# A decoder trunk on one core: the forget gate's columns in V's tiles, recurrent gates in plain float32, and another list for attention's entry

## The chip, the cores and the metric

The kernel runs on one core of one Trainium2 chip. A core has TensorE (in the views PE for its matmuls, PEld for its weight loads), VectorE (DVE), ScalarE (ACT), GpSimd (POOL) and SyncE (SP), which issues most DMAs. The metric is the time of one execution in device microseconds. The time of before is the median of three runs.

## The reference

Two layers over 256 positions of 1024 features. Each layer is a half-step SwiGLU FFN (1024 to 2816 and back), a token mixer and a second FFN, each with an RMS norm before and after it. The mixer of layer 0 is recurrent, that of layer 1 is attention with a forget gate, whose K, V and gate sum come from the stream between the layers.

```python
# layer 0's mixer; 1344 channels, 16 blocks of 84
gate, rec = split(hn @ w_in)
rec = causal_depthwise_conv(rec, conv_w, conv_b)           # 4 taps
r = sigmoid(blockwise(rec, w_a) + b_a);  i = sigmoid(blockwise(rec, w_x) + b_x)
log_a = -8 * r * softplus(-lam);  a = exp(log_a)
u = sqrt(-expm1(2 * log_a)) * (i * rec)
h_t = a_t * h_(t-1) + u_t                                   # a scan over the positions
m = (gelu(gate) * h) @ w_out
# shared by layer 1, from z = rms_norm(h, kv_norm_g)
k, v = split(z @ w_kv);  c = cumsum(log_sigmoid(z @ w_f + b_f))    # w_f: 1024 x 16
# layer 1's mixer, causal, 16 heads of 64
logits = q k^T / 8 + c_q - c_k;  m = softmax(logits) v @ w_o
```

## The kernel before, in words

**Split matmuls.** A float32 weight tile `raw` (128 x up to 1024) is split by `split` (L169) into a high part `whi`, which ACT copies with rounding to float32r (L178), and a low part `wlo`, which DVE gets by subtraction (L179). Activations are split in the same way (`xhi`, `xlo`; `zhi`, `zlo`; `hhi`, `hlo`; `yh`, `yl`). `mm3` (L184 to L188) forms a product from three float32r matmuls with the activation stationary: hi by hi, hi by lo, lo by hi. `mm3w` (L190 to L195) does so with the weight stationary. Attention's logits (L970) and values (L997) are plain float32 matmuls.

**Items and slots.** The weights form a list of items; each has a `prep` (load and split) and a `work` for the token tiles t = 0 and t = 1 (128 positions each). `slot(t, i)` does one item's work and then a `tick`. `run` lets t = 0 go ahead of t = 1 by up to `LAG` = 7 items. There are 3 buffers for raw tiles and 10 for split ones (`RAW`, `WB`); `prepare_next` prepares an item when the one ten before it is done for both token tiles. A tick counts down what `defer(n, fn)` has postponed by n ticks, prepares an item and issues some of `queue`, in which each entry has a cost in us; up to `SHARE` = 0.8 us of cost is issued per tick, and `flush(key)` issues all up to the last entry of a key. The order of PE's instructions is that of the program; the order of the other engines is set by a scheduler when the kernel is built.

**Ends of sub-layers.** `row_items` (L395) runs the products that go back to 1024 columns, in two PSUM banks of 512 columns. For t = 1 its last `rows` items are done bank by bank. Then `enter` (L247) takes square sums of both banks (ACT, L208), rstd (POOL, L201 and L203), adds to the stream `h` (DVE, L260), and defers the transposes and splits that make the next inputs: `inputs` by 3 ticks (L217), or `norm`, by 1 tick, which normalises h first (`stat`, then `hn`, L277) and defers the transposes `go` (L284) by 2 more. `norm` is used at the end of the first FFN, ahead of the recurrent stage.

**The recurrent stage** follows a list written by hand, `RG_ORDER` (L818): `0g3` is gate unit 3 for t = 0 (columns of `gate`, in groups of 504, 504 and 336; 2 or 3 k-tiles per unit), `r2` makes two 126-channel tiles of `rec` for all 256 positions, `gw2` is the blockwise gates of that pair. `conv` (L631): ACT writes `xc` from PSUM, DVE adds three taps (L647), ACT makes `ch` (L649), DVE `cl` (L652). A gw unit loads eight small blocks, splits them as a weight tile, does 8 products of 256 columns with `mm3w` and takes tanh (L694). `after_gates` queues L711 (scale and shift, DVE), tanh (L714), exp (L715), L716 and a Newton step (L720 to L725) for expm1's accuracy. For every two pairs `batch` queues the square roots (L739), u (L744, L745), the scans (L749), the transposes of the gate columns (L757) and their gelu (L759), the product (L771), and its split (`yh` L773, `yl` L778). `w_out` follows as `row_items` whose row k needs batch k // 4.

**K, V and the forget gate.** `post_f` and `work_f` (L897, L933): V's first half as four items of 512 columns, the forget gate as one item with 16 columns and 8 k-tiles, V's second half, then K. Both read `zx`, which `enter` of the second FFN makes as the first of two destinations.

**Attention** follows `ATT_ORDER` (L1045): `0` and `1` are the next item of that token tile (8 of w_q, then 8 of w_o), `a0` and `a1` the next step of the attention of that tile. Step i issues logits i, values i - 3, transposes i - 2 and, at two places, an output. `heads_T` (L869) makes q's transposes by deferring two `turn`s by 2 and 3 ticks.

Of the kernel before, what the change touches and what calls it, by code (L numbers as in the profile page):

```python
# [44 lines left out]
def trunk_kernel(ctx: ExitStack, tc: tile.TileContext, A: dict, out: bass.AP):  # L45
# [201 lines left out]
    def enter(t, dests, pf, gb, half, last=False, normed=False):  # L247
# [24 lines left out]
        def norm():  # L272
            stat(t)
            hn = []
            for n in range(2):
                hn.append(hpool.tile([P, 512], F32, tag="t1", name=nm("hn"), bufs=2))
                nc.vector.tensor_scalar(hn[n], h[t][:, n * 512:(n + 1) * 512], rs[t][:, 0:1], None, ALU.mult)  # L277

            def go():
                tps = []  # L280
                for n in range(2):
                    tp = gtbank()
                    for j in range(4):
                        nc.tensor.transpose(tp[:, j * P:(j + 1) * P], hn[n][:, j * P:(j + 1) * P], ident)  # L284
# [110 lines left out]
    def row_items(w, widths, get_x, post, rows=1):  # L395


        acc = {}
        kept = []
        nk = len(widths)  # L400
        r0 = 0
        for k, kp in enumerate(widths):
            def prep(kp=kp, r0=r0):
                return split(load_raw(w[r0:r0 + kp, :], kp, D), kp, D)

            def work(t, u, k=k):
                if k == 0:
                    acc[t] = [mmbank(), mmbank()]
                if t == 1 and k >= nk - rows:
                    kept.append((k, u))  # L410
                    if k < nk - 1:
                        return
                    todo = [(kk, uu, n) for n in range(2) for (kk, uu) in kept]
# [19 lines left out]
    def ffn_items(pool_of, wg, wu, wd, post_g, next_dests, last=False, normed=False):  # L433
# [55 lines left out]
        row_items(wd, [P] * 22, lambda t, k: (hid[t][0][:, k, :], hid[t][1][:, k, :]), post_down, 4 if last else 1)  # L489
# [46 lines left out]
    sp2 = rw.tile([RT, NRT], F32, name="sp2")  # L536

# [7 lines left out]
    def rg_params():  # L545
# [8 lines left out]
        def rest():  # L554
# [3 lines left out]
            nc.vector.tensor_scalar(sp2, sp, 2.0, None, ALU.mult)  # L558
        defer(1, rest)

# [14 lines left out]
    xcs, chs, tt, th, yy = {}, {}, {}, {}, {}  # L575

    def add_gate_unit(g, k0, kn):
# [5 lines left out]
        def work(t, u):  # L583
# [6 lines left out]
            if k0 + kn == 8:  # L590
                tok = pools["r"].tile([P, 4 * RT], F32, tag="tok", name=nm("tok"), bufs=4)
                nc.scalar.activation(tok[:, :nn], ps, AF.Copy)
                toks[(g, t)] = tok
# [37 lines left out]
    def conv(p, ps):  # L631
        tl, w = tiles_of(p), pw(p)
        m = len(tl)
# [3 lines left out]
        ch = pools["r"].tile([RT, 2, S], F32R, tag="ch", name=nm("ch"), bufs=2)  # L637
        cl = pools["r"].tile([RT, 2, S], F32R, tag="cl", name=nm("cl"), bufs=2)
        xcs[p], chs[p] = xc, (ch, cl)
# [4 lines left out]
        def taps(j, i):  # L644
# [4 lines left out]
            nc.scalar.activation(ch[:w, j, :], xc[:w, j, :], AF.Copy)  # L649

        def low():
            nc.vector.tensor_tensor(cl[:w, :m, :], xc[:w, :m, :], ch[:w, :m, :].bitcast(F32), ALU.subtract)  # L652

        first = [(1.25, ("c", p), lambda j=j, i=i: taps(j, i)) for j, i in enumerate(tl)] + [(0.65, ("c", p), low)]
# [3 lines left out]
    def add_gw_unit(p):  # L658
        tl, w = tiles_of(p), pw(p)
        m = len(tl)  # L660
        n = m * RT if m == 2 else BLK

        def prep():
            raw = new_raw()
            v = raw[:w, :2 * m * n]
# [11 lines left out]
            return split(v, w, 2 * m * n)  # L677

        def work(t, u):
# [3 lines left out]
            ch, cl = chs[p]  # L683
# [16 lines left out]
        rg[f"gw{p}"] = len(items)  # L700
        items.append((prep, work))

    def after_gates(p):
# [3 lines left out]
        t_ = tt[p][:w, :m, :] if p in tt else None  # L707

        def zz():
            for j, i in enumerate(tl):  # L710
                nc.vector.tensor_scalar(th[p][0][:w, j, :], th[p][0][:w, j, :], sp2[:w, i:i + 1], sp2[:w, i:i + 1],  # L711
                                        ALU.mult, ALU.add)
            tt[p] = pools["r"].tile([RT, 2, S], F32, tag="tt", name=nm("tt"), bufs=6)
            nc.scalar.activation(tt[p][:w, :m, :], z, AF.Tanh)  # L714
            nc.scalar.activation(z, z, AF.Exp, scale=-2.0)  # L715
# [3 lines left out]
        def newton():  # L719
            nc.vector.tensor_scalar(z, z, 0.5, 0.5, ALU.mult, ALU.add)  # L720
            nc.vector.scalar_tensor_tensor(b, tt[p][:w, :m, :], 1.0, z, ALU.add, ALU.mult)
# [6 lines left out]
        queue.extend([(1.1 * s, ("n", p), zz), (1.0 * s, ("n", p), newton), (1.0 * s, ("n", p), newton2)])  # L728
# [3 lines left out]
    def batch(g):  # L732

        pairs = [p for p in (2 * g, 2 * g + 1)]

        def roots():
            for p in pairs:
                v = tt[p][:pw(p), :len(tiles_of(p)), :]
                nc.scalar.activation(v, v, AF.Sqrt)  # L739

        def u_of(p):
            w, m = pw(p), len(tiles_of(p))
            v = tt[p][:w, :m, :]
# [3 lines left out]
        def scan(p, j):  # L747
            w = pw(p)
            nc.vector.tensor_tensor_scan(tt[p][:w, j, :], th[p][0][:w, j, :], tt[p][:w, j, :], 0.0, ALU.mult, ALU.add)  # L749

        def gelu(t):
            tok = toks[(g, t)]
            tp = trbank()
            y = pools["r"].tile([RT, 4, P], F32, tag="y", name=nm("y"), bufs=2)
# [3 lines left out]
            for (a, b, w) in parts_of(g):  # L758
                nc.scalar.activation(y[:w, a:b, :], tp[:w, a * P:b * P].rearrange("p (a b) -> p a b", a=b - a),  # L759
                                     AF.Gelu_apprx_tanh)  # L760
            ys[(g, t)] = y

        def product(t):
            y = ys[(g, t)]
            if t not in yy:
                yy[t] = (pools["r"].tile([RT, NRT, P], F32R, name=f"yh{t}"), pools["r"].tile([RT, NRT, P], F32R, name=f"yl{t}"))
            yh, yl = yy[t]
            for jj, p in enumerate(pairs):
                w, m = pw(p), len(tiles_of(p))
                v = y[:w, 2 * jj:2 * jj + m, :]  # L770
                nc.vector.tensor_tensor(v, v, tt[p][:w, :m, t * P:(t + 1) * P], ALU.mult)  # L771
            for (a, b, w) in parts_of(g):
                nc.scalar.activation(yh[:w, 4 * g + a:4 * g + b, :], y[:w, a:b, :], AF.Copy)  # L773

        def low(t):
            y, (yh, yl) = ys[(g, t)], yy[t]
            for (a, b, w) in parts_of(g):
                nc.vector.tensor_tensor(yl[:w, 4 * g + a:4 * g + b, :], y[:w, a:b, :],  # L778
                                        yh[:w, 4 * g + a:4 * g + b, :].bitcast(F32), ALU.subtract)
# [7 lines left out]
        q.insert(2, (0.0, key, lambda: gelu(0)))  # L787
        q.insert(3, (0.0, key, lambda: gelu(1)))
# [5 lines left out]

    ys = {}
# [7 lines left out]
    add_rec_units(0)  # L803
    add_rec_units(1)
    add_gw_unit(0)
    add_rec_units(2)
    add_gw_unit(1)
    add_rec_units(3)
    add_gw_unit(2)
    for k0 in (0, 3, 6):  # L810
        add_gate_unit(2, k0, min(3, 8 - k0))
    add_rec_units(4)
    add_gw_unit(3)
    add_rec_units(5)
    add_gw_unit(4)
    add_gw_unit(5)
# [11 lines left out]
    def get_yy(t, k):  # L828
        flush(("y", k // 4))
        w = width(k)  # L830
        return yy[t][0][:w, k, :], yy[t][1][:w, k, :]
# [60 lines left out]
    def post_v(n):  # L892
        def f(t, ps):
            nc.scalar.activation(kv["v"][t][:, n * 512:(n + 1) * 512], ps, AF.Copy, scale=rs[t][:, 0:1])
        return f

    def post_f(t, ps):  # L897
# [8 lines left out]
        def rest():  # L906
# [5 lines left out]
            defer(9, lambda: running(t))  # L912
# [13 lines left out]
    proj_items(A["w_kv"], D, 512, z_x, post_v(0))  # L926

    def prep_f():
        raw = new_raw()
        nc.sync.dma_start(raw[:, :P].rearrange("p (k n) -> p k n", k=8), A["w_fgate"].rearrange("(k p) n -> p k n", p=P))  # L930
        return split(raw[:, :P], P, P)

    def work_f(t, u):  # L933
        ps = mmbank()[:, :NH]
        for k in range(8):
            mm3(ps, *z_x(t, k), u.hi[:, k * NH:(k + 1) * NH], u.lo[:, k * NH:(k + 1) * NH], k == 0, k == 7)
        post_f(t, ps)

    items.append((prep_f, work_f))
    proj_items(A["w_kv"], D + 512, 512, z_x, post_v(1))  # L940
# [92 lines left out]
    for n in range(2):  # L1033
# [11 lines left out]
    ATT_ORDER = ("0 0 0 0 0 0 0 0 a0 1 a0 1 1 a0 1 a0 1 a0 1 a0 1 a0 a1 1 a0 a1 "  # L1045
                 "0 a1 0 a1 0 a1 0 a1 0 a1 0 a1 0 a1 0 a1 1 a1 1 a1 1 1 1 1 1 1")
# [29 lines left out]
    run(n_ffn1, lag_in=3)  # L1076
# [3 lines left out]
    for name in RG_ORDER:  # L1080
# [8 lines left out]
        else:  # L1089
            slot(None, rg[name])  # L1090
    state["a"] = state["b"] = n_rg
    run(n_wout)
# [61 lines left out]
```

## Time and profile before

| | |
|---|---|
| median of 3 runs (lowest to highest) | 1058.16 us (1056.62 to 1058.39) |
| the profiled execution: time, span | 1056.71 us, 1055.0 us |
| mean granted TensorE clock | 0.982 |
| first FFN ends, t = 0 and t = 1 | about 199 and 211 us |
| recurrent stage with w_out | about 211 to 346 us |
| V, forget gate and K | about 534 to 597 us |
| attention with w_q and w_o | about 781 to 861 us |

The span is the time from the first instruction to the last; 1.7 us of the execution lie outside it. Busy shares say how long an engine had an instruction in it. Matmuls are pipelined: a record of 0.39 us can be followed by the next after 0.23 us, so the rate of PE is read from one start to the next. "A <- B: x, n, m" in a list of waits says that A's engine sat idle for x us in all, n times, at longest m, until B was done. A granted clock of 0.90 over a stretch says that the throttle let TensorE have nine tenths of its full clock there, as a mean.

### The profile page before, as it was taken

To read this page: it belongs to the slowest core of one execution; us is meant where nothing else is said; L and a number is where in the kernel's file an instruction comes from. 1 tells how busy PE (TensorE), PEld (TensorE's weight loads), DVE (VectorE), ACT (ScalarE), POOL (GpSimd) and SP (SyncE) were. 2 spreads that over 40 slices of the span, in tenths; PEclk is the share of its full clock that TensorE was granted. 3 is DMA by queue.
4 is the path that set the end of the run, shared out by engine and by line. 5 is a ranking of instruction groups with operands and counts; after the bars stand their busy time and mean duration, and the time that the engine had idled before them with its cause. 6 is when DMAs were issued, how large, how long until landed. Compare 5 with 4: busy or idle time off the path is not lost.

```text
span 1055.0 us, 13090 instructions
## 1 busy us (share of the span) xinstructions
PE 1019.9 (97%) x4870; PEld 843.2 (80%) x4870; DVE 624.0 (59%) x771; ACT 539.3 (51%) x739; POOL 48.7 (5%) x109
## 2 busy tenths in 40 slices
PE   7999999989978999999999999999999999999997
PEld 4778888779966888888878888888888888888885
DVE  4666554548997755554486455555476475555542
ACT  3555543538886644443355444444357574454431
POOL 4200000010001100000010000000010010000000
PEclk9999999989988999999999999999999999999999
DMA  5776655536245676655446666655563156766541
GB/s 185 236 221 196 182 188 189 160 88 161 70 158 161 203 213 192 183 181 195 142 160 181 178 180 180 195 182 184 190 203 113 49 161 178 200 180 189 190 140 40
DMA packets 90742, 178.86 MB, mean 170 GB/s; under 512 B 11694, under 2 KB 28150, under 8 KB 90678
## 3 DMA queue, kind: packets, MB, share of 16 engines
q1 hardware_dynamic: 90006, 177.94, 55.9%
q8 instruction: 38, 0.62, 0.2%
q14 instruction: 26, 0.21, 0.1%
q0 software_dynamic: 640, 0.07, 0.1%
q10 hardware_dynamic: 32, 0.01, 0.0%
HBM read 176.95 MB, written 1.05 MB: 169 GB/s over the span
## 4 chain that ended last, share of the span: by engine, by line
PE 83%; DVE 6%; ACT 4%; DMA 4%; issue 2%; POOL 1%; DVEq 0%; SPq 0%; POOLq 0%; ACTq 0%
PE mm L186 25%; PE mm L188 25%; PE mm L187 25%; DVE wlo L179 3%; PE tr L462 2%; DMA raw<-in_ffn_w_gate_dram 2%; ACT whi L178 1%; PE mm L997 1%; PE gt L970 1%; ACT junk L208 1%; DMA raw<-in_ffn_w_up_dram 1%; PE gt L217 1%; PE tr L883 1%; PE mm L195 1%; PE mm L193 1%
## 5 line engine op out<-in xcount | busy, mean ns | idle before, releaser
L179 DVE TENSOR_TENSOR wlo<-raw,whi 128x1024 fp32r<-128x1024 f32 (+3 forms) x338 | 408.0, 1210 | 312.8 <-ACT whi L178 307.6
L178 ACT ACTIVATE whi<-raw 128x1024 fp32r<-128x1024 f32 (+2 forms) x332 | 348.6, 1052 | 359.9 <-PE mm L188 290.9
L186 PE MATMUL mm<-whi,xhi 128*128 128x512 f32 (+2 forms) x784 | 312.3, 398 | 5.3 <-ACT xhi L229 3.3
L187 PE MATMUL mm<-wlo,xhi 128*128 128x512 f32 (+2 forms) x784 | 306.4, 391 | 1.5 <-DVE wlo L179 1.5
L188 PE MATMUL mm<-whi,xlo 128*128 128x512 f32 (+2 forms) x784 | 306.5, 391 | 0.0
L186 PEld LDWEIGHTS mm<-whi,xhi 128*128 128x128 f32 x784 | 148.6, 189 | 35.2 <-POOL whi L176 3.4
L188 PEld LDWEIGHTS mm<-whi,xlo 128*128 128x128 f32 x784 | 148.3, 189 | 31.7 <-DVE xlo L232 0.6
L187 PEld LDWEIGHTS mm<-wlo,xhi 128*128 128x128 f32 x784 | 148.7, 190 | 30.5 <-DVE wlo L179 2.1
L186 PE MATMUL mm<-whi,hhi 128*128 128x512 f32 x352 | 139.5, 396 | 0.0
L188 PE MATMUL mm<-whi,hlo 128*128 128x512 f32 x352 | 139.0, 395 | 0.0
L187 PE MATMUL mm<-wlo,hhi 128*128 128x512 f32 x352 | 138.7, 394 | 0.0
L188 PEld LDWEIGHTS mm<-whi,hlo 128*128 128x128 f32 x352 | 66.1, 188 | 15.4
L187 PEld LDWEIGHTS mm<-wlo,hhi 128*128 128x128 f32 x352 | 66.1, 188 | 15.3
L186 PEld LDWEIGHTS mm<-whi,hhi 128*128 128x128 f32 x352 | 66.1, 188 | 15.1
L456 DVE SCALAR_TENSOR_TENSOR prod<-mm,rstd,sil 128x512 f32<-128x512 f32 (+1 forms) x48 | 33.9, 705 | 37.8 <-PE mm L188 34.0
L447 ACT ACTIVATE sil<-mm,rstd 128x512 f32<-128x512 f32 (+1 forms) x48 | 31.3, 651 | 44.9 <-PE mm L188 44.9
L201 POOL TENSOR_SCALAR nv<-ss 128x1 f32<-128x1 f32 x24 | 9.4, 391 | 759.6 <-ACT junk L208 759.6
L256 DVE TENSOR_TENSOR t<-mm,gb 128x512 f32<-128x512 f32 x24 | 16.3, 688 | 31.1 <-ACT junk L208 30.8
L466 ACT ACTIVATE hhi<-tr 128x512 fp32r<-128x512 f32 (+1 forms) x48 | 26.6, 553 | 14.6 <-PE tr L462 14.5
L467 DVE TENSOR_TENSOR hlo<-tr,hhi 128x512 fp32r<-128x512 f32 (+1 forms) x48 | 30.5, 642 | 3.4 <-ACT hhi L466 1.5
L208 ACT ACTIVATE junk<-mm 128x512 bf16<-128x512 f32 x24 | 14.2, 592 | 33.2 <-PE mm L188 32.8
L186 PE MATMUL mm<-whi,zhi 128*128 128x512 f32 (+1 forms) x80 | 31.0, 387 | 0.0
(178 smaller groups left out, 950.7 us busy)
## 6 DMA issues: line engine op xcount, KB each, us to landing
raw<-in_ffn_w_down_dram SPq DMA_DIRECT2D x88, 512.0 KB
raw<-in_ffn_w_up_dram SPq DMA_DIRECT2D x80, 512.0 KB
raw<-in_ffn_w_gate_dram SPq DMA_DIRECT2D x78, 512.0 KB
raw<-in_rg_w_in_dram SPq DMA_DIRECT2D x20, 504.0 KB
raw<-in_w_kv_dram SPq DMA_DIRECT2D x16, 512.0 KB
raw<-in_ffn_w_gate_dram SPq DMA_DIRECT2D x20, 256.0 KB
raw<-in_rg_w_out_dram SPq DMA_DIRECT2D x10, 504.0 KB
raw<-in_ffn_w_up_dram SPq DMA_DIRECT2D x16, 256.0 KB
```

What stands on the lines that cost most here:

```text
L178: nc.scalar.activation(hi[:parts, c:c + m], rawv[:, c:c + m], AF.Copy)
L179: nc.vector.tensor_tensor(lo[:parts, c:c + m], rawv[:, c:c + m], hi[:parts, c:c + m].bitcast(F32), ALU.subtract)
L186: nc.tensor.matmul(ps, xh, wh, start=first, stop=False)
L187: nc.tensor.matmul(ps, xh, wl, start=False, stop=False)
L188: nc.tensor.matmul(ps, xl, wh, start=False, stop=last)
L208: nc.scalar.activation(junk[:, :src.shape[1]], src, AF.Square, scale=f, accum_out=acc)
L256: nc.vector.tensor_tensor(t1[n], pf[n], gb[:, n * 512:(n + 1) * 512], ALU.mult)
L447: nc.scalar.activation(s[:, :nn], ps, AF.Silu, scale=rs[t][:, 0:1])
L456: nc.vector.scalar_tensor_tensor(pr[:, :nn], ps, rs[t][:, 0:1], s, ALU.mult, ALU.mult)
L462: nc.tensor.transpose(tp[:, j * P:(j + 1) * P], pr[:, j * P:(j + 1) * P], ident)
L466: nc.scalar.activation(hv, tp[:, :nn], AF.Copy)
L467: nc.vector.tensor_tensor(lv, tp[:, :nn], hv.bitcast(F32), ALU.subtract)
```

## The change

- *Forget gate.* The item of its own goes. V's columns are cut into 344, 340 and 340; the first group's tiles carry the 16 forget columns behind their 344, by a second DMA. Each item has two k-tiles, so there are 12 where there were 9. `post_f` reads the last 16 columns of the first group's bank.
- *Recurrent stage.* The gates are plain float32 matmuls of the unsplit weight block and of `xc`; `ch`, `cl` and the split of the gate weights go. The blocks are loaded in the first FFN, into six buffers `gy`, which later hold `yh` and `yl`. Scale and shift of L711 move into ACT's tanh and exp, one per 126-channel tile (`sp2`, and `sp4` = -4 `sp`). Gelu is taken as the gate columns leave PSUM, for two token tiles together where their units lie apart; the transposes come after the scans and the product reads them from PSUM. The Newton step stays.
- *Orders.* `RG_ORDER` and `ATT_ORDER` change, `OUT_ORDER` replaces `run` for w_out.
- *Ends of sub-layers.* `rows` becomes 2, for t = 0 also. `norm` is called at once, sums squares by halves, and defers the transposes by 5. The first FFN ends with a lag of 8.

```diff
         def norm():
-            stat(t)
+            ss = new_ss()
+            for n in range(2):
+                square_sum(h[t][:, n * 512:(n + 1) * 512], ss[:, n:n + 1])
+            rs[t] = rstd_of(ss, 2)
...
-            defer(2, go)
+            defer(5, go)
...
-            defer(1, norm)
+            norm()
...
-                if t == 1 and k >= nk - rows:
-                    kept.append((k, u))
+                m = rows if t == 1 else min(rows, 2)
+                if k >= nk - m:
+                    kept[t].append((k, u))
...
-                nc.scalar.activation(tok[:, :nn], ps, AF.Copy)
+                if (g, t) not in ((0, 1), (2, 0)):
+                    for gg, tt_ in {(1, 1): [(0, 1)], (2, 1): [(2, 0)]}.get((g, t), []) + [(g, t)]:
...
+                        nc.scalar.activation(tok[:, :n], gacc[(gg, tt_)][:, :n], AF.Gelu_apprx_tanh)
...
-            nc.scalar.activation(ch[:w, j, :], xc[:w, j, :], AF.Copy)
-
-        def low():
-            nc.vector.tensor_tensor(cl[:w, :m, :], xc[:w, :m, :], ch[:w, :m, :].bitcast(F32), ALU.subtract)
...
-            raw = new_raw()
-            v = raw[:w, :2 * m * n]
+            v = box["w"] = rw.tile([P, 1024], F32, tag="gy", name=nm("gw"), bufs=6)[:w, :2 * m * n]
             nc.gpsimd.memset(v, 0.0)
...
-            return split(v, w, 2 * m * n)
...
-                        mm3w(ps[:w, j * S:(j + 1) * S], u.hi[:, o:o + w], u.lo[:, o:o + w], ch[:w, k, :], cl[:w, k, :],
-                             k == 0, k == m - 1)
+                        nc.tensor.matmul(ps[:w, j * S:(j + 1) * S], wv[:, o:o + w], xc[:w, k, :],
+                                         start=k == 0, stop=k == m - 1)
...
+        ahead(20 + 6 * p, prep)
...
-                nc.vector.tensor_scalar(th[p][0][:w, j, :], th[p][0][:w, j, :], sp2[:w, i:i + 1], sp2[:w, i:i + 1],
-                                        ALU.mult, ALU.add)
-            nc.scalar.activation(tt[p][:w, :m, :], z, AF.Tanh)
-            nc.scalar.activation(z, z, AF.Exp, scale=-2.0)
+            for (dst, f, c) in ((t_, AF.Tanh, sp2), (th[p][0], AF.Exp, sp4)):
+                for j, i in enumerate(tl):
+                    nc.scalar.activation(dst[:w, j, :], th[p][0][:w, j, :], f, bias=c[:w, i:i + 1], scale=c[:w, i:i + 1])
...
-        q.insert(2, (0.0, key, lambda: gelu(0)))
-        q.insert(3, (0.0, key, lambda: gelu(1)))
+        q.append((0.0, key, lambda: (gate_T(0), gate_T(1))))
...
-    RG_ORDER = ("0g0 0g1 0g2 0g3 0g4 0g5 0g6 0g7 r0 1g0 1g1 1g2 1g3 r1 gw0 1g4 1g5 r2 gw1 1g6 1g7 r3 gw2 "
-                "0g8 0g9 0g10 r4 gw3 1g8 r5 gw4 1g9 1g10 gw5").split()
+    RG_ORDER = ("0g0 0g1 0g2 0g3 0g4 0g5 0g6 0g7 r0 1g0 1g1 1g2 r1 gw0 1g3 1g4 r2 gw1 1g5 1g6 r3 gw2 1g7 "
+                "0g8 0g9 0g10 r4 gw3 r5 1g8 1g9 gw4 1g10 gw5").split()
+    OUT_ORDER = [0] * 8 + [1] * 4 + [0] * 3 + [1] * 7
...
-            defer(9, lambda: running(t))
+            defer(15, lambda: running(t))
...
+    VCOLS = [(0, 344), (344, 340), (684, 340)]
...
-    ATT_ORDER = ("0 0 0 0 0 0 0 0 a0 1 a0 1 1 a0 1 a0 1 a0 1 a0 1 a0 a1 1 a0 a1 "
-                 "0 a1 0 a1 0 a1 0 a1 0 a1 0 a1 0 a1 0 a1 1 a1 1 a1 1 1 1 1 1 1")
+    ATT_ORDER = ("0 0 0 0 0 0 0 0 a0 1 a0 1 1 1 a0 1 a0 1 a0 1 a0 a1 1 a0 "
+                 "0 a1 a0 a1 0 a1 0 a1 0 a1 0 a1 0 a1 0 a1 0 a1 1 a1 1 a1 1 1 1 1 1 1")
...
-    run(n_ffn1, lag_in=3)
+    run(n_ffn1, lag_in=3, lag_out=8)
```

More of the change, by code (lines that the diff above doesn't have):

```diff
@@ L536, in trunk_kernel @@
     sp2 = rw.tile([RT, NRT], F32, name="sp2")
+    sp4 = rw.tile([RT, NRT], F32, name="sp4")
     def rg_params_load():
@@ L574, in trunk_kernel @@
     toks = {}
[L575 removed]
+    xcs, tt, th, yy = {}, {}, {}, {}
     def add_gate_unit(g, k0, kn):
@@ L648, in taps, with gw_unit @@
                                                par[:w, k * NRT + i:k * NRT + i + 1], xc[:w, j, s:], ALU.mult, ALU.add)
-            nc.scalar.activation(ch[:w, j, :], xc[:w, j, :], AF.Copy)
-        def low():
-            nc.vector.tensor_tensor(cl[:w, :m, :], xc[:w, :m, :], ch[:w, :m, :].bitcast(F32), ALU.subtract)
-        first = [(1.25, ("c", p), lambda j=j, i=i: taps(j, i)) for j, i in enumerate(tl)] + [(0.65, ("c", p), low)]
+        first = [(1.25, ("c", p), lambda j=j, i=i: taps(j, i)) for j, i in enumerate(tl)]
         n = max([i for i, q in enumerate(queue) if q[1][0] == "c"], default=-1)
         queue[n + 1:n + 1] = first
-    def add_gw_unit(p):
+    def gw_unit(p):
         tl, w = tiles_of(p), pw(p)
@@ L699, in work @@
             after_gates(p)
-        rg[f"gw{p}"] = len(items)
-        items.append((prep, work))
+            tick()
+        ahead(20 + 6 * p, prep)
+        gw[p] = work
     def after_gates(p):
@@ L734, in batch @@
         pairs = [p for p in (2 * g, 2 * g + 1)]
+        tps, ys = {}, {}
         def roots():
-            for p in pairs:
-                v = tt[p][:pw(p), :len(tiles_of(p)), :]
+            for (a, b, w) in parts_of(g):
+                v = tt[g][:w, a:b, :]
                 nc.scalar.activation(v, v, AF.Sqrt)
@@ L748, in scan, with gate_T @@
             w = pw(p)
-            nc.vector.tensor_tensor_scan(tt[p][:w, j, :], th[p][0][:w, j, :], tt[p][:w, j, :], 0.0, ALU.mult, ALU.add)
-        def gelu(t):
+            v = tt[g][:w, 2 * (p % 2) + j, :]
+            nc.vector.tensor_tensor_scan(v, th[p][0][:w, j, :], v, 0.0, ALU.mult, ALU.add)
+        def gate_T(t):
             tok = toks[(g, t)]
-            tp = trbank()
-            y = pools["r"].tile([RT, 4, P], F32, tag="y", name=nm("y"), bufs=2)
+            tp = tps[t] = trbank()
             for j in range(len(pairs) * 2 if g < 2 else 3):
@@ L757, in gelu, with product, low @@
                 nc.tensor.transpose(tp[:w, j * P:(j + 1) * P], tok[:, j * RT:j * RT + w], ident)
-            for (a, b, w) in parts_of(g):
[L759 to L771, printed above, removed]
-            for (a, b, w) in parts_of(g):
[L773 to L779, printed above, removed]
+        def product(t):
+            y = ys[t] = pools["r"].tile([RT, 4, P], F32, tag="y", name=nm("y"), bufs=2)
+            if t == 0:
+                yy[g] = [rw.tile([P, 1024], F32R, tag="gy", name=nm("y"), bufs=6).rearrange("p (t a b) -> p t a b", t=2, a=4)
+                         for _ in range(2)]
+            for (a, b, w) in parts_of(g):
+                tp = tps[t][:w, a * P:b * P].rearrange("p (a b) -> p a b", a=b - a)
+                nc.vector.tensor_tensor(y[:w, a:b, :], tp, tt[g][:w, a:b, t * P:(t + 1) * P], ALU.mult)
+                nc.scalar.activation(yy[g][0][:w, t, a:b, :], y[:w, a:b, :], AF.Copy)
+        def low(t):
+            yh, yl = yy[g]
+            for (a, b, w) in parts_of(g):
+                nc.vector.tensor_tensor(yl[:w, t, a:b, :], ys[t][:w, a:b, :], yh[:w, t, a:b, :].bitcast(F32), ALU.subtract)
         key = ("y", g)
@@ L802, in trunk_kernel @@
             add_gate_unit(g, k0, 2)
[L803 to L809, printed above, removed]
+    for p in range(4):
+        add_rec_units(p)
     for k0 in (0, 3, 6):
@@ L924, in z_x, with v_items, prep, work @@
         return zx[t][0][:, k, :], zx[t][1][:, k, :]
[L926 to L940, printed above, removed]
+    VCOLS = [(0, 344), (344, 340), (684, 340)]
+    def v_items(c0, n, extra):
+        nn = n + extra
+        acc = {}
+        for k0 in range(0, 8, 2):
+            def prep(k0=k0):
+                raw = new_raw()
+                v = raw[:, :2 * nn].rearrange("p (k n) -> p k n", k=2)
+                rows = slice(k0 * P, (k0 + 2) * P)
+                nc.sync.dma_start(v[:, :, :n], A["w_kv"][rows, D + c0:D + c0 + n].rearrange("(k p) n -> p k n", p=P))
+                if extra:
+                    nc.sync.dma_start(v[:, :, n:], A["w_fgate"][rows, :].rearrange("(k p) n -> p k n", p=P))
+                return split(raw[:, :2 * nn], P, 2 * nn)
+            def work(t, u, k0=k0):
+                if k0 == 0:
+                    acc[t] = mmbank()
+                ps = acc[t][:, :nn]
+                for j in range(2):
+                    k = k0 + j
+                    mm3(ps, *z_x(t, k), u.hi[:, j * nn:(j + 1) * nn], u.lo[:, j * nn:(j + 1) * nn], k == 0, k == 7)
+                if k0 == 6:
+                    if extra:
+                        post_f(t, ps[:, n:])
+                    nc.scalar.activation(kv["v"][t][:, c0:c0 + n], ps[:, :n], AF.Copy, scale=rs[t][:, 0:1])
+            items.append((prep, work))
+    for i, (c0, n) in enumerate(VCOLS):
+        v_items(c0, n, NH if i == 0 else 0)
     for n in range(2):
@@ L1089, in trunk_kernel @@
         else:
-            slot(None, rg[name])
-    state["a"] = state["b"] = n_rg
-    run(n_wout)
+            gw[int(name[2:])]()
+    nxt = [n_rg, n_rg]
+    for t in OUT_ORDER:
+        slot(t, nxt[t])
+        nxt[t] += 1
+    state["a"], state["b"] = nxt
     rcm.__exit__(None, None, None)
```

49 lines of the change are left out of this document (22 added, 27 removed).

## The prediction

> **What bounds the kernel now.** I read the page first (busy shares, then the slices), then a table of stretches, then who PE waited for, then the chain and the timeline where the change works.
>
> ```profile
> PE 1019.9 (97%) x4870; PEld 843.2 (80%) x4870; DVE 624.0 (59%) x771; ACT 539.3 (51%) x739; POOL 48.7 (5%) x109
> ...
> PE   7999999989978999999999999999999999999997
> ...
> PEclk9999999989988999999999999999999999999999
> ```
>
> TensorE is in use nearly always, so time can come from three places only: less matmul work, PE's waits, or stretches of lowered clock. Both show in the 9th, 12th and 13th of 40 slices (PE 8, 7, 8, and PEclk 8 in each). The table of stretches (length, then busy time of PE, PEld, DVE, ACT, POOL, then granted clock):
>
> ```profile
> 204.00:226.00 22.00, 17.14 (x72) 13.80 (x71) 16.08 (x22) 9.93 (x16) 4.25 (x7) 0.84 0.63 173
> ...
> 246.00:288.00 42.00, 42.00 (x326) 41.03 (x325) 39.22 (x71) 38.44 (x63) 3.06 (x4) 1.00 0.43 110
> 288.00:328.00 40.00, 28.28 (x127) 22.27 (x126) 38.77 (x71) 34.50 (x53) 0.00 (x0) 0.87 0.51 160
> 331.00:523.00 192.00, 192.00 (x871) 157.89 (x870) 108.08 (x108) 93.20 (x109) 5.58 (x15) 1.00 0.63 188
> 534.00:567.00 33.00, 31.62 (x153) 26.21 (x152) 23.49 (x54) 16.89 (x28) 3.88 (x6) 0.90 0.49 154
> ```
>
> The FFN stretch (331 to 523) has no gap. The recurrent stage has: from 246 to 328 DVE is busy 78.0 of 82 us while PE idles 11.7, so there VectorE is the bound. Who PE waited for (total us, times, longest):
>
> ```profile
> PE mm L186 <- ACT yh L773: 6.8, 2, 4.4
> PE gt L284 <- DVE hn L277: 4.9, 2, 3.6
> PE gt L194 <- DVE cl L652: 4.4, 1, 4.4
> ...
> PE gt L217 <- DVE h L260: 1.7, 2, 1.3
> ...
> PE gt L970 <- ACT qT L884: 1.3, 1, 1.3
> ```
>
> **Part by part.** The sum goes against the profiled execution: span 1055.0, 1.7 more around it, 1056.7; the median of the runs shown is 1058.2, so 1.4 is added at the end. Rates of PE come from start to start in the timeline and the chain:
>
> ```profile
> 268.15 0.29 PE L193 MATMUL gt<-ch,whi 126*126 126x256 f32 x1
> ...
> 271.01 0.32 PE L186 MATMUL mm<-whi,xhi 128*128 128x336 f32 x1
> ...
> 542.48 0.17 PE L186 MATMUL mm<-whi,zhi 128*128 128x16 f32 x1
> ...
> 545.08 0.48 PE L186 MATMUL mm<-whi,zhi 128*128 128x512 f32 x1
> ```
> ```profile
> 819.36 0.87 PE gt L970 x4
> ```
>
> *Gates in plain float32: +3.0.* One gate pair's 24 split matmuls of 256 columns take 271.01 - 268.15 = 2.86 us, 0.119 each; a product is three, 0.357. There are 42 products (five pairs of 8, one of 2): 15.0 us. Plain float32 with 256 columns is in the trace as attention's logits: four records, two products, 0.87 us, so 0.435 each, 18.2 us in all. Its 66 rows are the nearest form to 126 rows; bounds are 0.42 (the best pairs) and 0.476 (four times 0.119), +2.6 to +5.0. On PE this part loses. The Trainium skill ("FP8 and Floating Point Precision", TensorE Precision Notes) says against it that true float32 makes four passes through the array; by four passes of the split rate the part would cost +5.0 and the sum come out 2.0 later. The logits' two records of 0.217 lie between.
>
> *The recurrent stage's vector work: -13.6.* Groups of the stretch 230 to 330 (count | busy us, mean ns | idle before):
>
> ```profile
> L711 DVE TENSOR_SCALAR th<-th,sp 126x256 f32<-126x256 f32 (+1 forms) x11 | 4.6, 417 | 0.2 <-ACT th L694 0.2
> ...
> L652 DVE TENSOR_TENSOR cl<-xc,ch 126x512 fp32r<-126x512 f32 (+1 forms) x6 | 3.8, 640 | 0.2 <-ACT ch L649 0.2
> ```
>
> Off DVE go these 17, and the low parts of the gates' weights (five wlo of 1.20, one of 0.32: 6.3). That is 14.7 of busy time, some 13 without the 0.08 us by which neighbours overlap. The products read PSUM (one 126x512 at the 0.69 of such rows for two of 0.41): nothing. Off ACT go the 11 ch (4.6), the weights' high parts (5 x 1.05 + 0.35), the 8 gelus behind the transposes (3.2; six token copies become gelus at their length) and some 3 of 14 table loads of 1.283 (tanh runs with gelu's table and with exp's); on go 1.9 us of tanh and exp cut in halves: about 13 less.
> So from 246 to 328 DVE would have 65 us and PE 70.3 - 5.9 (halved clock) + 3.0 = 67. The two are close, so not every wait goes. What falls away: 11.7 us of waits (L773 6.8, L652 4.4, wlo 0.5) and the three stretches of halved clock behind them, 5.9. What is late next: the taps for gw4, then batch 1's yh for row 4 of w_out (before 2.6 late), then batch 2's for row 8 (4.6 late). gw4 comes 9.0 us of PE work behind r4 (gw3 3.5, r5 2.8, two gate units 2.8); the taps cost DVE 2.4 and ACT 0.9. Row 8 has 12 slots of 1.40 ahead of it by OUT_ORDER, 16.8 us, where there were 10; its chain after gw5 (tanh, exp with a table load, Newton, sqrt with a load, u, scans, product, copy, low) adds up to 12 to 13 from these rows' means, and DVE has some 5 wlo of 1.2 and batch 1's 2.4 to do beside it. I leave 4 us late of 17.6: -13.6; bounds -6 (twelve late, as DVE at 95% of its time leaves little) and -17.6.
>
> *Entry of the recurrent stage: -6.0.* PE waits 1.2 and 3.6 us for hn, and the clock is halved after it, 2.6 more: 7.5. Now the transposes stand five slots behind the end instead of four (1.4 us more cover each), and the square sum goes by halves, so 0.45 less lies behind the last h. The first wait is covered. The second chain took 8.8 us from the last matmul (211.0) to hn (219.8), with ACT's splits inside it; five slots are 6.9. It stays about 1.5 late, too short for a halved clock (1.2 to 1.4 us waits at 204.0 and 800.7 left it at 1.0). Bounds 0 and -7.5. gw's loads move into the first FFN: a memset of 0.94 on POOL, idle there, and 8 issues of 0.43 on SP, 3.4 us per pair, ahead of a weight load. There loads are issued about 8 us before their split and land in some 4.5, and PE has three units of 2.8 us ready: nothing. Without that cover 3 us per pair, 18 in all.
>
> *Forget gate in V's tiles: -6.3.* The 16-column matmuls take 545.08 - 542.48 = 2.60 us per token tile for 24, 5.2 in both. V's 96 of 512 columns take 0.233: 22.4. Between 336 columns (0.1535) and 512 the step is 0.45 ns a column: 340 is 0.155, 360 is 0.164. After: 16 x 3 x (0.164 + 2 x 0.155) = 22.8. So -4.8. The clock also falls to half in the windows right behind both 16-column bursts (546.1 and 563.2, 3.4 us each, 0.90 over the stretch): -3.3. Against it: token tile 1's entry stands three slots behind the FFN's end, and a slot shrinks from 1.40 to 0.98, so the wait of 1.3 on L260 grows by 1.3; and behind the transposes, four slots of 0.96 wait for zlo, which took 5.1 us: about 1.2 late; rows=2 gives bank 0 away 0.7 earlier: +1.8. Bounds +0.5 and +4 (with a halved window). More items (12 for 9) cost splits of 0.8 instead of 1.05; ACT and DVE have room there (16.9 and 23.5 of 33).
>
> *Attention's list: -1.3.* One more slot stands between the last turn of q's heads and logits 2, so the L970 wait goes; the first o slot needs only output 0, four entries back. Bounds 0 and -1.3. *rows=2 elsewhere: -0.3* of the last L260 wait (0.4).
>
> Sum: 3.0 - 13.6 - 6.0 - 6.3 - 1.3 - 0.3 = -24.5: 1032.2, and 1033.6 on the median.
>
> **Rivals.**
> *VectorE stays the bound.* The wlo of w_out and the scans keep yh late, as DVE's 65 of 67 us allow: only 5 of the 17.6 come back, 1042.2. For it: DVE at 39.2 of 42 even while PE had no wait. Against: ACT is relieved as well, and batch 2 gets two more slots.
> *New waits at the entries.* The entry of the recurrent stage keeps 4 more, and the short V slots end in a halved clock, 3.4 more: 1041. For it: ACT's splits (1.05 each) stood inside both chains, and stay. Against: the first has 1.4 us more cover, the second gets bank 0 earlier.
> *Slower: the clock halves under the gates.* If plain float32 counts as little work for the clock, as the 16-column matmuls seem to, the stretch from gw0 to gw5, 60 us of PE work, takes 120, and hides the 4 late: 1033.6 + 60 - 4 = 1089.6. It decides from 49 us at half clock on, which eat the 24.5. Against: attention's float32 logits and values (802 to 850) run at 1.0. The Trainium skill ("TensorE: Matmul & The Clock Gate", Part 1) has the clock halved after an idle window of 3.4 us; the windows of 3.4 agree, but PE was busy all through the burst at 542.5, so idleness alone isn't what is counted here.
> *Float32 isn't float32.* If the plain gates ran as one split-rate pass, 42 x 0.119 = 5.0: 1033.6 - 13.2 = 1020.4. Against: the logits' two records.
>
> **How the numbers follow.** Forecast 0.62 (own range 1027 to 1040), VectorE 0.20, entries 0.10, clock 0.06, one pass 0.02. The bounds of the terms sum to 1026 and 1053. With the middle rivals at 1041 and 1042 and as much again around them as around the forecast, the range that leaves out under 2 in 10 is 1025 to 1046; its last us below is for the one-pass case. What a measurement tells from no change is about 0.2%, 2 us. Faster: all but the clock case (slower, 0.06) and a corner beyond 1053, where several bounds fail together (same, 0.02): 0.92.
>
> **What would show it.** Two records of about 0.217 for each gate product; no L652, L711, L649; PE's waits on yh below 4 us together and clock 1.0 from 290 on; hn's second wait near 1.5; no 128x16 matmuls in mm, no halved windows there, L260's wait near 2.5; no wait on qT. I am wrong if DVE still fills the stage and yh's waits stay, if the clock drops inside a gw burst, or if whi in the first FFN begins to wait for DMA.

## The result, and the profile after

After takes 1031.42 us (median of four runs, 1030.42 to 1033.83), before, measured beside it, 1057.62 (the three runs shown above and a fourth): a ratio of 0.9756 (95% interval 0.9737 to 0.9776). The profiled execution took 1033.83 us, its span 1032.1. The same lines of the page as before:

```profile
PE 1006.6 (98%) x4828; PEld 835.1 (81%) x4828; DVE 609.9 (59%) x748; ACT 533.9 (52%) x732; POOL 48.6 (5%) x109
...
PE   7999999999999999999999999999999999999997
...
PEclk9999999999999999999999999999999999999999
```

The three slices with 7 and 8 are gone, in PE's row and in the clock's. The stretches that answer to those of before, with the same columns; V, K and the forget gate now lie at 515 to 576:

```profile
204.00:226.00 22.00, 20.99 (x101) 16.95 (x100) 18.41 (x24) 14.55 (x25) 2.98 (x6) 1.00 0.67 202
246.00:288.00 42.00, 42.00 (x285) 39.64 (x284) 37.23 (x62) 40.00 (x60) 0.00 (x0) 1.00 0.44 140
288.00:328.00 40.00, 37.32 (x179) 30.71 (x178) 36.51 (x61) 32.67 (x50) 2.54 (x6) 1.00 0.40 121
...
515.00:576.00 61.00, 58.13 (x316) 51.23 (x315) 43.89 (x85) 34.39 (x52) 2.66 (x11) 1.00 0.65 202
```

From 288 to 328 TensorE is busy 37.32 of 40 us where it was 28.28, at full clock. VectorE is still busy 36.51 there: its share alone would hardly tell that it has ceased to be the bound. What PE still waits for:

```profile
PE gt L694 <- issue: 1.9, 1, 1.9
...
PE tr L874 <- DVE htok L863: 1.7, 1, 1.7
PE gt L217 <- DVE h L260: 1.7, 2, 1.1
...
PE gt L287 <- DVE hn L280: 1.0, 1, 1.0
PE mm L188 <- DVE y L778: 0.7, 1, 0.7
PE mm L1000 <- ACT pT L991: 0.3, 1, 0.3
```

The waits of 6.8 for yh, 4.4 for cl, 4.9 for hn and 1.3 for qT have gone or shrunk; two are new: htok, and one ahead of the last gates (L694). The profile names no releaser for the latter ("issue"). By the timeline these gates start at 296.26, 0.1 us after the first two tanh of the pair before (L698, 295.32 to 296.16), which stand behind a table load at 294.03; so I read it as a wait for the PSUM bank that those tanh free. The stages, cut at the last matmul of each, in the profiled executions (us):

| | before | after | difference |
|---|---|---|---|
| start and first FFN | 210.5 | 212.5 | +2.0 |
| recurrent stage and w_out | 135.6 | 117.4 | -18.1 |
| second FFN | 187.9 | 189.0 | +1.1 |
| V, forget gate, K | 63.1 | 56.8 | -6.3 |
| third FFN | 183.9 | 183.9 | 0 |
| attention | 79.2 | 78.5 | -0.8 |
| fourth FFN | 187.9 | 187.1 | -0.8 |

The +2.0 is no part of the change: in the ten kernels below that share after's first FFN it ends between 208.6 and 211.9 us, so this profile lies above most of them. Two waits near its start, for xhi (4.1 us, before 3.3) and prod (2.0, before 0.7), make up 2.1.

### The profile page after: what moved, and what is told of

Read it like the earlier page. It is cut to its first block, busy times and chain, and to the rows that moved or that the text cites. A ratio compares the mean times of both kernels' runs of the same rounds, so it can differ in the third digit from the quotient of the medians.

```text
span 1032.1 us, 12938 instructions
## 1 busy us (share of the span) xinstructions
PE 1006.6 (98%) x4828; PEld 835.1 (81%) x4828; DVE 609.9 (59%) x748; ACT 533.9 (52%) x732; POOL 48.6 (5%) x109
## 4 chain that ended last, share of the span: by engine, by line
PE 78%; ACT 7%; DMA 7%; DVE 4%; issue 2%; POOL 1%; SPq 0%; DVEq 0%; POOLq 0%; ACTq 0%
PE mm L188 24%; PE mm L187 24%; PE mm L186 24%; DMA raw<-in_ffn_w_gate_dram 3%; DVE wlo L179 2%; ACT whi L178 2%; PE tr L466 2%; DMA raw<-in_ffn_w_up_dram 1%; DMA raw<-in_rg_w_in_dram 1%; PE gt L973 1%; PE mm L1000 1%; ACT junk L208 1%; DMA raw<-in_rg_w_out_dram 1%; DMA raw<-in_w_kv_dram 1%; ACT th L698 1%
## 5 line engine op out<-in xcount | busy, mean ns | idle before, releaser
L179 DVE TENSOR_TENSOR wlo<-raw,whi 128x1024 fp32r<-128x1024 f32 (+5 forms) x335 | 401.8, 1203 | 300.7 <-ACT whi L178 294.6
L178 ACT ACTIVATE whi<-raw 128x1024 fp32r<-128x1024 f32 (+4 forms) x329 | 343.6, 1046 | 352.3 <-PE mm L188 276.3
L188 PEld LDWEIGHTS mm<-whi,hlo 128*128 128x128 f32 x352 | 66.1, 188 | 15.4
L186 PEld LDWEIGHTS mm<-whi,hhi 128*128 128x128 f32 x352 | 66.1, 188 | 14.8
L470 ACT ACTIVATE hhi<-tr 128x512 fp32r<-128x512 f32 (+1 forms) x48 | 26.6, 553 | 14.6 <-PE tr L466 14.5
L466 PE MATMUL tr<-ident,prod 128*128 128x128 f32 x176 | 27.0, 272 | 2.0 <-DVE prod L460 2.0
```

The costliest lines, as they stand in the source:

```text
L178: nc.scalar.activation(hi[:parts, c:c + m], rawv[:, c:c + m], AF.Copy)
L179: nc.vector.tensor_tensor(lo[:parts, c:c + m], rawv[:, c:c + m], hi[:parts, c:c + m].bitcast(F32), ALU.subtract)
L186: nc.tensor.matmul(ps, xh, wh, start=first, stop=False)
L188: nc.tensor.matmul(ps, xl, wh, start=False, stop=last)
L466: nc.tensor.transpose(tp[:, j * P:(j + 1) * P], pr[:, j * P:(j + 1) * P], ident)
L470: nc.scalar.activation(hv, tp[:, :nn], AF.Copy)
```

## The experiments

Names with u_ undo something in after, e_ and x_ alter after, b_ does one part in before. "Stage" is the recurrent stage with w_out (before 135.6, after 117.4). Ratios are to before in the same session (1055.9 to 1056.5); differences (+6.4) are to after's 1031.42, measured in another session; before's own medians differ by 1.8 from session to session, so a difference of 1 or 2 us here says little. Stages come from one profiled execution each. The code is shortened: `...` and plain names like `hi` and `lo` stand for longer expressions.

**u_vec**: the vector work back, its results unread by the gates (`ch`, `low` and the scale and shift of the old L711).

```
+ nc.scalar.activation(ch[:w, j, :], xc[:w, j, :], AF.Copy)
+ nc.scalar.activation(hi[:w, :n2], v, AF.Copy)      # the gate weights; each followed by DVE's subtraction
```

> The kernel after, with the vector work of before put back beside it and PE's work as after: ACT makes ch, DVE subtracts (into the same tile), the gate weights are split on ACT and DVE, and L711 with whole-tile tanh and exp stands again; the split results are used by nobody. Theory (the recurrent stage gained because DVE and ACT got less to do): 10 us slower than after (7 to 14), with PE's waits on yh back. Rival (the lists, the later transposes and the buffers did it): 0 to 3 slower.

Measured: 1037.79 (ratio 0.9814, 0.9770 to 0.9858), stage 123.7: +6.4. VectorE is as busy in the stage as in before (109.3 us, before 110.1, after 97.9), yet of the waits only these grew much (after has 1.9 and 1.0), and two halved windows cost 3.4 us; the wait for y is 0.4, so yh's waits of before are not back:

```profile
PE gt L709 <- issue: 3.7, 1, 3.7
...
PE gt L287 <- DVE hn L280: 2.8, 1, 2.8
```

So the amount of vector work is about a third of the stage's 18, below what the theory gave.

**u_gates**: the same work, and the gates as split products that read it.

```
- nc.tensor.matmul(ps[...], wv[:, o:o + w], xc[:w, k, :], ...)
+ mm3w(ps[...], hi[:, o:o + w], lo[:, o:o + w], ch[:w, k, :], cl[:w, k, :], ...)   # hi, lo in the ring of split tiles
```

> The kernel after with the gates as split matmuls again: the same vector work as in u_vec, but its results are used, so PE has 42 x 3 split matmuls instead of 42 plain float32 ones. Theory: float32 costs PE some 2.4 us (84 records in 17.3 against 15.0), so this is about 2 faster than u_vec, that is 8 slower than after (5 to 12). Rival (lists and buffers did it, float32 only costs): 0 to 2.4 faster than after.

Measured: 1046.22 (0.9898, 0.9860 to 0.9936), stage 131.0: +14.8, above either. The old waits are back, in size too, and from 288 us on 10.3 us of PE's work ran in windows of halved clock, which costs some 5.2:

```profile
PE mm L186 <- ACT y L793: 8.9, 1, 8.9
PE gt L194 <- DVE cl L664: 4.0, 2, 2.7
```

**u_chain**: u_vec, with the gates reading a tile that stands behind ACT's `ch` and one DVE operation, so the path to their start is as long as with `ch` and `cl`. (`ch` is plain float32 here, its records read f32 to f32, so nothing is rounded to float32r; the "slightly rounded xc" of the expectation doesn't apply.)

```
+ nc.vector.tensor_tensor(ch[:w, :m, :], xc[:w, :m, :], ch[:w, :m, :], ALU.max)
- nc.tensor.matmul(ps[...], wv[...], xc[:w, k, :], ...)
+ nc.tensor.matmul(ps[...], wv[...], ch[:w, k, :], ...)
```

> u_vec, but the plain float32 gates read a tile that comes out of the chain ACT ch, then DVE (the larger of xc and its rounded copy, so the gates see a slightly rounded xc), as the split gates' operands did. It separates what u_gates (stage from the first FFN's end to w_out's end 131.0 us, after 117.4) and u_vec (123.7) mixed. Theory (the gates' start, two steps later, is the second half of the gain: 131.0 + 2.4 of dearer matmuls against 123.7): stage 129 to 134, some 8 slower than u_vec. Rival (in u_gates the split weights took buffers from the ring of weights): stage 123 to 126, as u_vec.

Measured: 1036.86 (0.9822, 0.9795 to 0.9848), stage 125.1, as the rival had it: the longer path alone didn't make u_gates slow. Two short waits for y lie close together here, and a halved window follows them (318.6 to 322.0):

```profile
PE mm L188 <- DVE y L795: 1.0, 1, 1.0
...
PE mm L186 <- ACT y L790: 0.5, 1, 0.5
```

**u_ring**: u_gates, with plain float32 products.

```
- mm3w(ps[...], hi, lo, ch, cl, ...)
+ nc.tensor.matmul(ps[...], (hi, lo)[k].bitcast(F32), (ch, cl)[k].bitcast(F32), ...)
```

> u_gates (split copies of the weights in the ring of split tiles, ch and cl for xc, the old scale and shift), but with its products as plain float32 matmuls that read these copies, high or low by turns; so the gates are not computed rightly, only their form, buffers and order are those of u_gates. It tells what made u_gates 7.3 us longer in the recurrent stage than u_vec, which had the same vector work unread. Theory: products that must wait for the copies and hold their buffers: stage 127 to 132 (u_gates 131.1), whole 1042 to 1046. Rival: the split matmuls themselves (their three records, their order among the others): stage 123 to 126 as u_vec (123.7) and u_chain (125.1), whole 1036 to 1039.

Measured: 1042.32 (0.9868, 0.9844 to 0.9892), stage 126.1. The stage lies at the rival's end, the median at the theory's (the profiled execution is the fastest of the four, 1.8 below the median): undecided. PE waits in the same places as u_gates, for less:

```profile
PE mm L186 <- ACT y L794: 4.4, 1, 4.4
...
PE gt L713 <- DVE cl L664: 3.2, 2, 2.2
```

From 288 us on halved windows take up 3.4 us here and 17.1 in u_gates; PE stands idle in 0.3 and 6.8 of them, so the clock costs some 1.6 and 5.2. Behind the longest wait for cl, 2.2 us here, it stays at 1.0; behind 2.7 in u_gates two windows of 3.4 are halved. So the 5 us between the two don't come from more TensorE work (u_gates has 3 less): longer waits (4.5 for y, 0.8 for cl) and the clock behind them (3.6) make them up. Why y is 4.5 later behind split products stays open.

**b_gates**: before, with the plain float32 gates alone (no `ch`, `cl`, split weights; old lists, old gelu, L711 and entry kept).

```
- mm3w(ps[...], u.hi[...], u.lo[...], ch[...], cl[...], ...)
+ nc.tensor.matmul(ps[...], wv[:, o:o + w], xc[:w, k, :], ...)
```

> The kernel before with one part alone: plain float32 gates on unsplit weights and xc (ch, cl and the split of the gate weights gone, two buffers for the blocks, loads where they were); L711, gelu, all lists and the rest as before. Theory (less vector work and the shorter chain to the gates are the gain, the lists little): 8 to 14 faster than before. Rival (it pays only with the new lists and early loads): 3 faster or less.

Measured: 1043.78 (0.9879, 0.9856 to 0.9902), stage 118.2. The whole gains 12.2 us by the medians, inside the theory's 8 to 14. The stage alone is 17.3 shorter, but that is too much to claim: the first FFN ends 2.8 later in this profile (213.3), mostly since the longer wait for hn and its halved window (207.2 to 210.6) now lie in it, where before had them in the stage (218.5 to 225.3). First FFN and stage together are 14.6 shorter. The dearer product on PE is the smaller side of it. L652's wait and all but 1.2 of L773's are gone, while the entry waits as it did in before:

```profile
PE gt L284 <- DVE hn L277: 5.0, 2, 2.8
...
PE mm L186 <- ACT yh L766: 1.2, 1, 1.2
```

**u_ord**: the old `RG_ORDER`, and `run` for `OUT_ORDER`.

> The kernel after with the order of the recurrent stage and of w_out as before (the old list, and run with its lag of 7). Theory (vector work): 0 to 4 slower, since row 8 of w_out has two slots less ahead of it. Rival (the lists did it): 8 or more slower.

Measured: 1032.51 (0.9769, 0.9733 to 0.9805), stage 119.8: +1.1, which the runs don't tell from nothing. The old list has 12 table loads in the stage where after has 15, and no wait at the gates. Of all waits on y and yh, the lists take off this one:

```profile
PE mm L186 <- ACT y L773: 2.6, 1, 2.6
```

**u_entry**: the entry as it was (`defer(1, norm)`, the square sum whole, `defer(2, go)`, the first FFN's lag 7).

> The kernel after with the entry of the recurrent stage as before: norm deferred by 1, its square sum in one piece, the transposes deferred by 2 more, the first FFN's lag 7. Theory: the second wait for hn is back at 3 to 4 us with a halved clock behind it, the first at about 1: 6 slower (3 to 7.5). Rival (the entry was late because of ACT's and DVE's load, which is gone): 0 to 2 slower.

Measured: 1037.54 (0.9818, 0.9802 to 0.9835), +6.1. The two waits (1.2 and 3.1) are back, and a halved window at 218.6 to 222.0:

```profile
PE gt L284 <- DVE hn L277: 4.3, 2, 3.1
```

**u_kv**: V in two halves of 512 and the forget gate as an item of its own, as in before.

> The kernel after with the forget gate as an item of its own and V in two halves of 512. Theory (work 4.8, halved clock 3.3, against 1.8 of longer waits): 6.3 slower, with the clock at half in one window behind each burst of 16-column matmuls. Rival (the halved windows of before had another cause): 3 slower and the clock at 1.0 there.

Measured: 1038.96 (0.9833, 0.9787 to 0.9880), +7.5; V to K takes 61.9 instead of 56.8. One window is halved behind the 16-column products (542.9 to 546.4), where before had two. The profiled execution is the fastest of the four, 3.2 below their median, so it shows less of the loss than the median has.

**e_nogelu**: after without gelu (the copy out of PSUM stays, as a plain copy). When ACT changes from one function to another, a table load of 1.283 us can stand between them (ACT_TABLE_LOAD). After has 15 in the stage, before had 14; by the line that follows, with count, busy us, mean ns:

```profile
L603 ACT ACT_TABLE_LOAD x5 | 6.4, 1283 | 0.1
L720 ACT ACT_TABLE_LOAD x5 | 6.4, 1283 | 0.1
...
L745 ACT ACT_TABLE_LOAD x3 | 3.8, 1283 | 0.1
...
L698 ACT ACT_TABLE_LOAD x2 | 2.6, 1283 | 0.0
```

Gelu (L603) stands alone five times, and tanh and exp (L720) have a load again behind each.

> The kernel after with the gate columns copied instead of put through gelu (gelu is left out of the computation), so that ACT has the same number of instructions but some 5 table loads of 1.283 less of 15. Theory (ACT is now the fuller engine of the stage, 52.4 of 56 us, and PE's wait of 1.9 before the last gates is for a bank that tanh frees behind a table load): 2 to 3 faster than after, that wait gone. Rival (ACT's loads lie beside other work): within 1.

Measured: 1030.43 (0.9752, 0.9736 to 0.9769), only 1.0 below after, as the rival had it. The stage itself bears out the theory: it falls to 114.1 (-3.4) with 6 loads, and L694's wait goes. Two of the 3.4 are given back at the turns of K's heads, where the wait grows and one window is halved behind it (551.3 to 554.7):

```profile
PE tr L874 <- DVE htok L863: 2.2, 1, 2.2
```

**e_twice**: every gate product twice.

```
- for j in range(m):
+ for j in [j for j in range(m) for _ in range(2)]:
```

> The kernel after, with every plain float32 gate product issued twice (the repeat starts the same sum anew, so the result is the same): 42 x 0.412 = 17.3 us more of TensorE work in the recurrent stage and nothing else. Theory: since the change TensorE is the bound of that stage (busy 113.8 of its 117.4 us, with 1.0 for hn, 1.9 for a bank and 0.7 for y as its only long waits), so at most these 3 us can hide something: the stage takes 131 to 135 and the whole 1045 to 1049, and the clock stays at 1.0 through bursts of twice the length. Rival: ScalarE or VectorE still sets the pace and TensorE merely follows it: half or more is hidden, stage 126 or less, whole 1040 or less.

Measured: 1045.67 (0.9906, 0.9874 to 0.9938), stage 132.3: it grew by 14.9. In it PE is busy almost throughout, at full clock, and only hn's wait (1.2) is left of the long ones:

```profile
212.00:343.00 131.00, 129.82 (x742) 115.43 (x741) 98.85 (x153) 92.45 (x138) 4.86 (x11) 1.00 0.45 130
```

**x_defer**: later transposes behind the FFNs and for the heads.

```
- defer(3, inputs)            - defer(2, lambda: turn(0)); defer(3, lambda: turn(1))
+ defer(4, inputs)            + defer(3, lambda: turn(0)); defer(4, lambda: turn(1))
```

> The kernel after, with the inputs at the end of an FFN deferred by 4 ticks instead of 3 and the two turns of the heads' transposes by 3 and 4 instead of 2 and 3. It aims at three waits that the profile of the changed kernel still has: 1.1 and 0.6 us for h ahead of the transposes at 522 and 334, and 1.7 for htok at 553. Theory: a slot of 0.96 to 1.4 us covers most of each, whole 1.5 to 3.4 shorter: 1028 to 1030. Rival: the chains behind (transposes, their splits, first use) become late by as much, since their own users stay where they are: 1031 to 1033.

Measured: 1033.75 (0.9790, 0.9765 to 0.9815), slower than both ranges. The second FFN and V to K gain 0.5 and 0.7, and attention loses 3.4: the same `heads_T` makes q's turns, and there the users stay where they were.

```profile
PE gt L973 <- ACT qT L875: 1.6, 2, 0.9
PE mm L1000 <- ACT pT L991: 1.5, 2, 1.2
```

**x_late**: x_defer, with gelu behind the transposes as before the change.

```
- nc.scalar.activation(tok[:, :n], gacc[...], AF.Gelu_apprx_tanh)
+ nc.scalar.activation(tok[:, :nn], ps, AF.Copy)     # gelu: tp to y, ahead of the product
```

> x_defer, and gelu moved back to where it stood before the change: the gate columns are copied out of PSUM when they are ready, and gelu follows the transposes, ahead of the product. Beside x_defer this is that one part of the change alone. Theory: gelu at the early place costs table loads (15 in the stage, 6 without any gelu, 3.4 us in all) and the 1.9 us wait for a bank behind one of them; with gelu in three bunches the stage is 1 to 2.5 shorter than in x_defer. Rival: at the late place gelu's two table loads of 1.28 lie in the chain from the last gates to y, and y is late again: a wait on y or yh of 1 to 3 us and a stage longer by 0 to 3.

Measured: 1031.39 (0.9765, 0.9737 to 0.9792), 2.4 below x_defer; stage 116.0, 12 loads, no wait at the gates, 0.4 and 0.6 for y. The two intervals overlap, and the stages (118.2 and 116.0) are one profile each: 1.7 of their 2.2 are a halved window in x_defer (293.3 to 296.7) behind a wait of 2.0 at the gates, where after's wait of 1.9 had none. So of the parts undone here, the early gelu is the only one that the kernel seems better without, by a little. After with late gelu and the old turns wasn't run; by the stages (attention 3.5 shorter, V to K 0.7 longer) it should be some 3 us below x_late, an estimate.

## Why the prediction was right, point by point

- **Gates, +3.0: right.** A burst of 8 products is 16 records:

```profile
241.16 3.62 PE L694 MATMUL gt<-xc,gw 126*126 126x256 f32 x16
244.42 0.60 PE L186 MATMUL mm<-whi,xhi 128*128 128x504 f32 x1
```

  Record to record is 0.216 us, and doubling a burst (e_twice) adds 3.45 for 8 products: 0.431 each, 18.1 for 42, +3.1. (The prediction's own 18.2 less 15.0 is 3.2, not 3.0.) Four times the split rate of 0.119, an estimate, would be 0.476, and no trace shows that. It doesn't speak against the four passes that the Trainium skill ("FP8 and Floating Point Precision", TensorE Precision Notes) names: 0.431 is four times 0.108, and no run here tells how long one pass takes.
- **Vector work, -13.6: the size right, the reason half right.** With the +3.0 of the gates it was to bring 10.6; b_gates, most of this part done alone, brought 12.2.

  I put all of it down to VectorE's and ScalarE's busy time. VectorE is busy 12.2 us less in the stage (110.1 to 97.9), close to the 13 forecast. ScalarE is busy 4.4 less (97.6 to 93.2), where I had about 13. Two steps failed there: of 14 table loads 3 were to go, and it is one more, since a gelu that follows its own unit stands between other functions; and tanh and exp in halves take 12.7 us where they took 7.2, +5.5 and not +1.9.

  The reason is half right because the same work put back unread (u_vec) costs the stage only 6.3. Read by the gates it costs 7.7 (u_chain), 8.7 (u_ring) or 13.6 (u_gates): the dependency adds 1.4 to 2.4, and the last 5 came with split products alone; that they lie in waits and the clock is shown, why the waits grow is not.

  4 us were to stay late; 1.9 and 0.7 did, and the 1.9 in a place that I hadn't named. The order was worth 2.4 of the stage (u_ord), 1.1 by the medians.
- **Entry, -6.0: right.** hn's second wait is 1.0 (forecast 1.5), without a halved window; undone, 6.1 come back by the medians, 3.8 of it in the stage by u_entry's profile.
- **Forget gate, -6.3: right in all (-6.3; 7.5 by u_kv's median), the waits in other places.** The forecast was 2.5 for h and 1.2 for zlo. It is 1.1 for h at 523 and 1.7 for htok at 555, against 1.35 in before: +1.5 for +1.8.
- **Attention, -1.3:** -0.8; qT's wait went, and pT's of 0.3 came. No run undoes this list alone.
- **The sum.** Against the profiled execution the forecast was -24.5. The two profiles differ by 22.9, with +2.0 in the first FFN, so the other stages give -24.9. The recurrent stage came out 2.7 better than the terms (3.0 - 13.6 - 6.0, of which the first wait of 1.2 lies in the first FFN: -15.4): 1.4 of smaller waits, 0.5 at the entry, 0.8 unassigned. The second FFN lost 1.1 that I had not counted, 0.6 of it a wait for h at 334, and the fourth gained 0.8. The median is 2.2 below the forecast of 1033.6, but no stage explains that: after's profile lies 2.4 above its own median, and before's 0.9 below the median of its four runs where I added 1.4. That the sum of the stages comes within 0.4 is in part luck, since the misses go both ways. By the medians the parts tried alone add up to 26.9 (gates 12.2, forget gate 7.5, entry 6.1, orders 1.1) against 26.2 for the whole.
- **The rivals.** VectorE as the bound fell by e_twice, where 14.9 of 17.8 us of added PE time (35.1 for 17.3, start to start) arrive. The halved clock under float32 fell: 1.00 in every stretch, with bursts of double length too. One pass fell by 0.431. New waits at the entries came true in part: 1.7 for htok, which at 2.2 in e_nogelu had a halved window behind it.

## What to carry to other kernels

A busy share of 90% beside an idle TensorE names a suspect, not the cause: put the work back unread and you see what its amount costs. Put it back as something that the matmuls read and you see more, but not one number: three ways of reading it cost 1.4, 2.4 and 7.3 us on top. Less work around a product can pay for a slower product: here 3 us more of matmul, and the whole 12 shorter. A gain read from one stage can have come from its neighbour, as in b_gates, so add up both sides of the border. An activation moved ahead "to where there is room" should be counted in table loads, 1.28 us each, in the order in which the scheduler will place it.

## What the runs showed of the hardware

Idle times of PE and the granted clock behind them, over all fourteen profiles from 150 us on: each of the 13 single waits of 2.4 us or more (2.41 to 8.9) has halved windows of 3.4 us beside it. Of those between 1.7 and 2.3 us three have one (1.74 in u_kv, 1.96 in x_defer, 2.22 in e_nogelu) and nine have none at once (1.89 in after, 2.26 in b_gates, for instance). And in u_chain a window is halved behind two waits of 0.53 and 1.01. So the length of one wait doesn't decide.

The idle time in the 3.4 us just before says more: ahead of each of these 17 it is 1.54 us or more (1.54 in u_chain). In b_gates the wait of 2.26 falls across an edge, if windows are counted on at 3.41 us from the halved one that ends at 210.6: 1.66 us lie in one window and 0.6 in the next. In the same way (counted back from 542.9) u_kv's wait of 1.69 at 520.6 lies in one window and halves nothing, while 1.78 us in the window before 293.8 of the same run do. By this counting, which is an estimate, the border lies near 1.5 to 1.8 us of idle time in a window of 3.4.

The Trainium skill ("TensorE: Matmul & The Clock Gate", Part 1) has the clock halved after an idle window of some 3.4 us, and the window free-running. The spread agrees with a place on such a grid; that waits of 1.74 to 3.3 us, none a whole window, are followed by a halved one differs from the page, and the runs decide.

The 16-column products halve the clock with PE busy, in before, u_kv and b_gates, but in u_kv once rather than twice; after, which carries their columns in wider tiles, has no halved window there.
